# Converting and subtracting w's blocks two at a time, with four moved steps in the prologue

## The chip, the cores and the metric

One core of one Trainium2 chip runs the whole problem in one launch. The metric is the device time of that launch in microseconds (us), as the median of several runs; the profiles are of single executions. Engines: PE is the matmul engine (TensorE), DVE the vector engine, ACT the scalar engine, POOL GpSimd, SP the engine whose queue issues the DMAs.

## The reference

```python
x: (8, 2048, 2048) float32     w: (2048, 2048) float32
cs = np.cumsum(x, axis=1)
diff = cs - (cs shifted by one row, zeros first)     # this is x again
return np.matmul(diff, w).astype(np.float32)
```

A running sum followed by its difference gives x back, so the kernel computes `out = x @ w`: 16384 rows by 2048 columns, with an inner dimension of 2048, float32 in and out.

## The kernel before

**Rows.** The 16384 rows are 128 tiles of 128 rows. Tiles 0 to 3 (`PLAIN = 4`) are multiplied plainly in bf16 while w is still being loaded. From tile 4 on, groups of four tiles (g, g+1, g+2, g+3) go through two nested levels of a Winograd form of Strassen's multiplication in float16, with a scale for each row of x and one for each column half of w. In the code `h = g + 2`; the tiles of the first group are 4 (g), 5, 6 (h) and 7 (h+1).

**w in place.** `W_all` holds all of w in SBUF as 8 rows k of four sections of 1024 float32 numbers. Section `(a, h)` of row k is the half h of the columns of w's row block `ko = 8*a + k`. Once a section is no longer needed in float32, it is scaled by `uinv` and written over itself in float16; that takes half its bytes, so the other half of each section has room for a difference. The four converted blocks are B11, B12, B21, B22, and the differences are T1 = B12 - B11, T2 = B22 - T1, T3 = B22 - B12, T4 = B21 - T2. Each of these eight is 8 pieces, one for each k; before, one DVE instruction made one piece (1024 numbers in each partition): `block` (line 341) for a conversion, line 506 for T1 and `lessen` (line 586) for T2 to T4.

**The prologue.** w's left column half (h = 0) comes first, then the right one (h = 1), each as 16 loads of 512 KB (`fetch`, line 258) on SP's queue. Each block is cast to bf16 on DVE (`cast`, line 266) into a ring of 7 tiles `wb`, and ACT finds its greatest size (`measure`, line 272). PE multiplies tiles 0 to 3 with it (`plain`, line 303). For the left half the order is one block for all four rows at a time up to block 13; then blocks 14 and 15 are done row by row, and each row's sums are copied out of PSUM (`plain_out`, by ACT and DVE in turns). For the right half (`bring(ko)`): load, cast, measure, and behind each a conversion of one piece of B11 or B21 on DVE (`turn_left(1)`); blocks 12 to 15 are done row by row (`finish_row`), with the conversions of B12 in twos between. When `ko` is 10, x's tile 4 is loaded and weighed by ACT (`weigh`), DVE works out its scale (`scale_of`, lines 141 and 143) and ACT narrows it to float16 (`narrow`, line 163). `greatest_of_w(h)` and `scale_of_w(h)` give w's scales by DVE and POOL.

**Around the first group.** `turn` (line 176) transposes a narrowed tile of x by DMA into one of four pairs of tiles `x00 ... x31`; tile 5 goes to `x20, x21`, tile 7 to `x30, x31`. Until then these hold results of the prologue that wait to be stored (`spare`, and `left_over`'s result in `x30`), so their stores come ahead of the transposes. `left_over` (line 457) is the one product of 16 matmuls that the left half leaves out (row 3, second bank). `group_plain` then runs the first group with level-one products of 16 matmuls each; `group_half` and the classes behind it run the second group and all later ones. All later groups follow a list of steps, `ORDER`, written out by hand (`P1.cg` copies a PSUM bank on ACT, `keep.C21h1` scales one bank into an SBUF tile on ACT).

**Order.** `after(engine, ...)` keeps each engine's instructions in the order of the code; engines wait for each other by semaphores that are put in where tiles are shared. A DMA also waits for the DMA eight places ahead of it on SP's queue, since eight semaphores are used in turn.

Of the kernel before, what the change touches and what calls it, by code (L numbers as in the profile page):

```python
# [10 lines left out]
def kernel(  # L11
# [6 lines left out]
    nc = tc.nc  # L18
    P = 128
    B, S, D = x.shape  # L20
# [3 lines left out]
    KO = K // P  # L24
    KH = KO // 2
    NH = N // 2
# [40 lines left out]

    def spare_of(i, k):
        return blocks[:, i // 2, i % 2, ds(k, 2), :, :]

    uw = const.tile([P, 2], f32, name="uw")
    uinv = const.tile([P, 2], f32, name="uinv")
# [9 lines left out]
    def bank(i):  # L82
        return psum.tile([P, NB], f32, name=f"b{i}")
# [101 lines left out]
    with ExitStack() as head:  # L185
# [151 lines left out]
        def block(dst, a, h, k, engine):  # L337
# [5 lines left out]
            else:  # L343
                after(
                    "act", lambda: nc.scalar.activation(dst[k], src, COPY, scale=uinv[:, h : h + 1])
                )

        def dummies(banks):
            for i in banks:
                after(  # L350
                    "pe",
                    lambda: nc.tensor.matmul(
                        bank(i), zeros[:, :P], zeros, start=True, stop=True
                    ),
                )
# [22 lines left out]
            for r in (2 * a, 2 * a + 1):  # L378
                plain(0, r, 0)
        measure(0, 0)  # L380
        for ko in range(1, KO - 2):
            if ko >= EARLY:
                cast(0, ko)
            measure(0, ko)
            q = (ko + 1) // KQ
            turning = ko % KQ == KQ - 1
            if turning:
                xb = cast_x(q)
            for r in range(PLAIN):
                if turning and r in (0, PLAIN - 1):  # L390
                    a = r // 2
                    turned(q, a, turn_x(xb, a, 7), "act")
                plain(0, r, ko)
        for ko in range(KO - 2, KO):
            cast(0, ko)
            measure(0, ko)
        for ko in range(AHEAD):
            fetch(1, ko)
            cast(1, ko)
        for r in range(PLAIN):  # L400
            for ko in range(KO - 2, KO):
                plain(0, r, ko)
            plain_out(0, r)
        greatest_of_w(0)
        for ko in range(AHEAD):
            measure(1, ko)
        ps = [[bank(2 * r + n) for n in here(1, r)] for r in range(PLAIN)]
        left = [(B, a, k) for a, B in enumerate((B11, B21)) for k in range(KH)]

        def turn_left(n):  # L410
            for _ in range(min(n, len(left))):
                B, a, k = left.pop(0)
                block(B, a, 0, k, "dve")

        def bring(ko):
            fetch(1, ko)
            cast(1, ko)
            measure(1, ko)
            if ko == AHEAD:
                scale_of_w(0)  # L420
            turn_left(1)
            if ko == 10:
                load(PLAIN, 0)
                load(PLAIN, 1)
                weigh(PLAIN)
                scale_of(PLAIN)
            if ko == 11:
                narrow(PLAIN)
# [18 lines left out]
        def finish_row(r):  # L447
            for ko in range(KO - KQ, KO):
                plain(1, r, ko)
            plain_out(1, r)  # L450
# [16 lines left out]
            rows = ds((PLAIN - 1) * P, P)  # L467
            after("sp", lambda: put(c, rows, ds(NB, NB), nc.sync))

        turn_left(KH)  # L470
        unit_of(PLAIN)
        turn(PLAIN)
        weigh(PLAIN + 2)
        finish_row(0)
        for k in range(KH):
            block(B12, 0, 1, k, "dve")
            if k == 1:
                scale_of(PLAIN + 2)
            if k % 2:
                if k // 2:  # L480
                    finish_row(k // 2)
        unit_of(PLAIN + 2)
        narrow(PLAIN + 2)
        there = xP.rearrange("p r k m -> p (r k m)")
# [3 lines left out]
        def stores(which):  # L488
            for c, rows, columns in which:
                after("sp", lambda: put(c, rows, columns, nc.sync))  # L490
# [8 lines left out]
        unit_of(PLAIN + 1)  # L499
        narrow(PLAIN + 1)  # L500
        turn(PLAIN + 1)
        stores(done[:3] + done[5:])
        left_over(bank(2))

        for k in range(KH):
            after("dve", lambda: nc.vector.tensor_tensor(T1[k], B12[k], B11[k], SUB))


    class Part:
# [70 lines left out]

    def half_of(t, i):
        return in_twos(t)[:, i]

    def lessen(dst, p, q):
        for k in range(len(dst)):
            after("dve", lambda: nc.vector.tensor_tensor(dst[k], p[k], q[k], SUB))

    def less(dst, p, q):
        if len(dst.shape) == 4 or len(p.shape) == 4 or len(q.shape) == 4:
# [88 lines left out]
    def group_plain(g, X, Y, Z, V):  # L678
        h = g + 2
        lg, lh, kg = (units(t)[0] for t in (g, h, g + 1))  # L680
        ug, uh, vg = (units(t)[1] for t in (g, h, g + 1))
        A11g, A12g = parts(g)
        A11h, A12h = parts(h)
        A21g, A22g = parts(g + 1)
        A21h, A22h = parts(h + 1)
        S1g, S1h = S1
        S2g, S2h, S3g, S3h, S4g, S4h = A11g, A11h, A21g, A21h, A12g, A12h
        load(g + 4, 0)
        load(g + 4, 1)
        product(X, A11g, B11, True)  # L690
        for k in range(3):
            block(B22, 1, 1, k, "act")
        C11g = pair()
        keeps(C11g, X, lg)
        weigh(h + 1)
        for k in range(3, KH):
            block(B22, 1, 1, k, "act" if k < 6 else "dve")
        product(V, A12g, B21, True)
        product(Y, A11h, B11, True)
        lessen(T2[:1], B22[:1], T1[:1])  # L700
        adds(C11g, V, lg)
        puts(C11g, g, 0)
        lessen(T2[1:2], B22[1:2], T1[1:2])
        total(S1g, A21g, A22g, ADD)
        total(S3g, A11g, A21g, SUB)
        total(S2g, S1g, A11g, SUB)
        scale_of(h + 1)
        unit_of(h + 1)
        narrow(h + 1)
        kh, vh = units(h + 1)  # L710
        turn(h + 1)
        lessen(T2[2:], B22[2:], T1[2:])
        product(Z, A12h, B21, True)
        C11h, C22g = (
            [
                inner[:, ds(j, 2), :].rearrange("p a n -> p (a n)").bitcast(f32)
                for j in (i, i + 2)
            ]
            for i in (12, 16)
        )  # L720
        keeps(C11h, Y, lh)
        product(V, S1g, T1, True)
        keeps(C22g, V, vg)
        load(h + 4, 0)
        total(S4g, A12g, S2g, SUB)
        product(X, S2g, T2, False)
        C12g = pair()
        keeps(C12g, X, ug)
        lessen(T3, B22, B12)
        product(V, S4g, B22, False)  # L730
        total(S1h, A21h, A22h, ADD)
        total(S3h, A11h, A21h, SUB)
        total(S2h, S1h, A11h, SUB)
        weigh(g + 4)
        scale_of(g + 4)
        unit_of(g + 4)
        narrow(g + 4)
        load(h + 4, 1)
        turn(g + 4)
        load(g + 5, 0)  # L740
        load(g + 5, 1)
        product(X, S3g, T3, False)
        adds(C11h, Z, lh)
        puts(C11h, h, 0)
        del free[-2:]
        adds(C12g, V, ug)
        puts(C12g, g, 1)
        product(Y, S2h, T2, False)
        C12h = pair()
        keeps(C12h, Y, uh)  # L750
        adds(C22g, X, vg)
        puts(C22g, g + 1, 1)
        del free[-2:]
        total(S4h, A12h, S2h, SUB)
        product(Z, S1h, T1, True)
        weigh(h + 4)
        lessen(T4[:4], B21[:4], T2[:4])
        scale_of(h + 4)
        unit_of(h + 4)
        lessen(T4[4:], B21[4:], T2[4:])  # L760
        C22h = pair()
        keeps(C22h, Z, vh)
        narrow(h + 4)
        weigh(g + 5)
        product(Y, S3h, T3, False)
        in_2.first()
        in_2.fourth()
        load(h + 5, 0)
        load(h + 5, 1)
        turn(h + 4, [0])  # L770
        scale_of(g + 5)
        unit_of(g + 5)
        adds(C22h, Y, vh)
        puts(C22h, h + 1, 1)
        product(Z, S4h, B22, False)
        in_2.third()
        adds(C12h, Z, uh)
        puts(C12h, h, 1)
        narrow(g + 5)
        weigh(h + 5)  # L780
        turn(h + 4, [1])
        turn(g + 5, [0])
        product(X, A22g, T4, False)
        C21 = pair()
        keeps(C21, X, kg)
        puts(C21, g + 1, 0)
        turn(g + 5, [1])
        product(Y, A22h, T4, False)
        less(in_3.Q1, in_3.t12, in_3.t11)
        scale_of(h + 5)  # L790
        unit_of(h + 5)
        C21 = pair()
        keeps(C21, Y, kh)
        narrow(h + 5)
        in_3.second()
        less(in_1.Q1, in_1.t12, in_1.t11)
        turn(h + 5)
        load(g + 8, 0)
        load(g + 8, 1)
        puts(C21, h + 1, 0)  # L800
# [462 lines left out]
    for b in range(-early, len(groups) - late):  # L1263
        for name, ahead in ORDER:
            i = b + ahead
            if 0 <= i < len(groups) and name in groups[i].do:
                if i == len(groups) - 1 and name in END_ORDER:
                    continue
                if i == 1 and name in before:
                    before[name]()  # L1270
                groups[i].do.pop(name)()
                for sooner in SOONER.get(name, ()) if i == len(groups) - 1 else ():
                    groups[i].do.pop(sooner)()
    for name in END_ORDER:
# [32 lines left out]
```

## Time and profile before

| what | before |
|---|---|
| median of 3 runs | 1451.99 us (1451.88 to 1452.24) |
| the profiled execution's own time | 1450.92 us |
| its span, first to last instruction | 1449.1 us |
| PE busy | 1439.1 us (99%), 6686 matmul records |
| DVE busy | 1318.3 us (91%) |
| ACT busy | 971.7 us (67%) |
| POOL busy | 43.5 us (3%) |
| granted PE clock | 1.000 |
| DMA | 351.58 MB, mean 243 GB/s |

Busy is the union of an engine's recorded instructions. A matmul's record lasts 379 ns while matmuls start about 216 ns apart, so PE can lose some 160 ns between two matmuls and still count as busy; short losses are read from the starts. The profiled execution's time is 1.8 us over its span, and 1.07 us under the median.

### The profile page before, as it was taken

What the parts mean: (1) busy time and instruction counts of PE and PEld (TensorE: products, weight loads), DVE (VectorE), ACT (ScalarE), POOL (GpSimd) and SP (SyncE); (2) the same over time, 40 slices, a digit from 0 to 9 for tenths busy, and PEclk for the clock granted to TensorE, in tenths of its full rate; (3) what the DMA queues carried; (4) which work ended last, traced back from release to release, by engine and by line L of the source; (5) the groups of instructions that cost most, each with busy time, mean ns of one, the idle gap of its engine ahead of it and who ended that gap; (6) DMA issues with size and microseconds to landing.
All of it is one profiled execution on the core that took longest, in us unless ns stands there. A gap on an engine that the chain in (4) does not pass through costs nothing.

```text
span 1449.1 us, 20194 instructions
## 1 busy us (share of the span) xinstructions
PE 1439.1 (99%) x6686; PEld 651.7 (45%) x6692; DVE 1318.3 (91%) x2309; ACT 971.7 (67%) x1473; POOL 43.5 (3%) x130
## 2 busy tenths in 40 slices
PE   8999999999999999999999999999999999999998
PEld 4444444444444444444444444444444444444443
DVE  5898899999999999999999999999999999999998
ACT  6987567766666776666666667666667766666662
POOL 0011000000000000000000000000000000000000
PEclk9999999999999999999999999999999999999999
DMA  9999788899888898888898878998878998889973
GB/s 363 371 246 294 202 232 237 234 258 246 231 220 241 243 248 243 231 234 239 248 250 232 235 232 235 263 236 237 228 234 239 253 239 235 224 244 247 254 201 126
DMA packets 378199, 351.58 MB, mean 243 GB/s; under 512 B 274800, under 2 KB 274800, under 8 KB 377968
## 3 DMA queue, kind: packets, MB, share of 16 engines
q1 hardware_dynamic: 378096, 350.31, 86.7%
q8 instruction: 52, 0.85, 0.2%
q14 instruction: 51, 0.42, 0.1%
HBM read 150.99 MB, written 134.22 MB: 197 GB/s over the span
## 4 chain that ended last, share of the span: by engine, by line
PE 93%; DMA 5%; DVE 1%; issue 0%; ACT 0%; SPq 0%; DVEq 0%; ACTq 0%
PE b L623 61%; PE b L604 31%; DMA W<-in_w_dram 4%; DMA x<-F 1%; DVE c L634 1%; PE b L303 0%; DVE x L594 0%; PE b L457 0%; DMA out_dram<-c 0%; DVE wb L266 0%; DVE W L341 0%; ACT c L631 0%; ACT F L163 0%; SPq L224 0%; DVE S L594 0%
## 5 line engine op out<-in xcount | busy, mean ns | idle before, releaser
L634 DVE SCALAR_TENSOR_TENSOR c<-b,of,c 128x512 f32<-128x512 f32 x790 | 573.6, 746 | 70.2 <-PE b L623 60.0
L604 PE MATMUL b<-W,x 128*128 128x512 f16 x2144 | 506.8, 379 | 0.2 <-DVE x L594 0.2
L631 ACT ACTIVATE c<-b,of 128x512 f32<-128x512 f32 x492 | 312.7, 680 | 223.0 <-PE b L623 117.2
L623 PE MATMUL b<-W,x 128*128 128x512 f16 x1904 | 455.0, 379 | 0.1
L163 ACT ACTIVATE F<-F,of 128x1024 f16<-128x1024 f32 x246 | 282.2, 1147 | 175.1 <-DVE of L143 172.9
L623 PEld LDWEIGHTS <-x 128*128 128x128 f16 x2500 | 244.6, 98 | 296.1 <-issue 1.9
L604 PEld LDWEIGHTS <-x 128*128 128x128 f16 x2144 | 209.7, 98 | 253.4 <-DVE x L594 0.7
L124 ACT ACTIVATE waste<-F 128x1024 uint8<-128x1024 f32 x246 | 259.3, 1054 | 8.7 <-DMA F<-in_x_dram 6.6
L623 PEld LDWEIGHTS <-inner 128*128 128x128 f16 x1644 | 160.9, 98 | 194.0 <-issue 0.2
L623 PE MATMUL b<-W,inner 128*128 128x512 f16 x940 | 241.2, 379 | 0.0
L594 DVE TENSOR_TENSOR x<-x,x 128x1024 f16<-128x1024 f16 (+1 forms) x390 | 227.2, 583 | 3.2
L623 PE MATMUL b<-flow,x 128*128 128x512 f16 x588 | 150.9, 379 | 0.1
L623 PE MATMUL b<-inner 128*128 128x512 f16 x472 | 121.1, 379 | 0.0
L947 DVE TENSOR_TENSOR flow<-W 128x2048 f16<-128x2048 f16 x88 | 107.0, 1216 | 0.0
L1040 DVE TENSOR_TENSOR b<-b,c 128x512 f32<-128x512 f32 x116 | 80.5, 694 | 13.4 <-PE b L623 13.4
L149 POOL TENSOR_SCALAR of<-uw,of 128x2 f32<-128x2 f32 x124 | 42.2, 354 | 1301.6 <-DVE of L141 719.3
L947 DVE TENSOR_TENSOR flow<-W,inner 128x2048 f16<-128x2048 f16 x58 | 70.8, 1220 | 0.0
L1033 ACT COPY c<-b 128x512 f32<-128x512 f32 x58 | 33.4, 576 | 52.1 <-PE b L623 46.6
L303 PE MATMUL b<-wb,xP 128*128 128x512 bf16 x234 | 53.5, 379 | 2.8 <-ACT wb L264 1.9
L594 DVE TENSOR_TENSOR inner<-x 128x512 f16<-128x512 f16 x117 | 49.3, 421 | 3.1 <-DMA x<-F 1.1
L1033 ACT COPY b<-b 128x512 f32<-128x512 f32 x87 | 51.2, 588 | 0.0
L594 DVE TENSOR_TENSOR inner<-x,inner 128x512 f16<-128x512 f16 x117 | 49.2, 421 | 2.0
(66 smaller groups left out, 516.6 us busy)
## 6 DMA issues: line engine op xcount, KB each, us to landing
F<-in_x_dram SPq DMA_DIRECT2D x246, 512.0 KB, 5.3
out_dram<-c SPq DMA_DIRECT2D x492, 256.0 KB, 3.1
W<-in_w_dram SPq DMA_DIRECT2D x32, 512.0 KB, 8.4
W<-in_x_dram SPq DMA_DIRECT2D x16, 256.0 KB, 7.8
x<-F SPq DMA_TRANSPOSE x246, 3.4
out_dram<-o SPq DMA_DIRECT2D x5, 256.0 KB, 7.6
out_dram<-wb SPq DMA_DIRECT2D x5, 256.0 KB, 3.5
xP<-in_x_dram SPq DMA_DIRECT2D x1, 1024.0 KB, 6.2
```

The lines of the kernel that those rows point to most:

```text
L124: lambda: nc.scalar.activation(waste, where[t][i], ABS, scale=1.0 / ROW, accum_out=sums_of[t][:, i : i + 1],),
L149: after("pool", lambda: nc.gpsimd.tensor_scalar(u, uw, m, None, MUL))
L163: lambda: nc.scalar.activation(narrowed(t)[:, ds(i * NH, NH)], where[t][i], COPY, scale=s),
L303: lambda: nc.tensor.matmul(ps[r][n], xP[:, r, ko, :], wb[h, ko][:, ds(n * NB, NB)], start=(ko == 0), stop=(ko == KO - 1),),
L594: after("dve", lambda: nc.vector.tensor_tensor(dst.all, p.all, q.all, op))
L604: said = nc.tensor.matmul(to[n], a[k], b[k][:, n, :], start=(first and k == 0), stop=(k == KH - 1), skip_group_check=True,)
L623: said = nc.tensor.matmul(to, a[k], b[k], start=(first and k == 0), stop=(k == 3), skip_group_check=True)
L631: after("act", lambda: nc.scalar.activation(c, p, COPY, scale=u))
L634: after("dve", lambda: nc.vector.scalar_tensor_tensor(c, p, u, c, MUL, ADD))
L947: after("dve", lambda: nc.vector.tensor_tensor(in_twos(flow), x, y, op))
L1033: after("act", lambda: nc.scalar.copy(c, p))
L1040: after("dve", lambda: nc.vector.tensor_tensor(t, p, s, ADD))
```

## The change

1. Conversions of B11, B21, B12 and of B22's last two pieces take two neighbouring k in one DVE instruction (`two_blocks`, 2048 numbers in each partition) instead of one. In `bring`, a pair comes behind every even `ko` (2 to 14) instead of one piece behind each; the last pair stands where the last piece stood.
2. T1, T2, T3 and T4 are made by `minus`, again two k to an instruction. T2's first two pieces are made together ahead of `adds(C11g, ...)`; before, one stood ahead of it and one behind.
3. The left half's row-by-row end starts with block 15 alone; block 14 joins the loop over all rows.
4. For the second group `keep.C21h1` is moved from its place in `ORDER` to right behind `P1.cg` of the third group; both are ACT's.
5. The stores at the end of the prologue: `left_over`'s goes first, then the other one out of an x tile (`done[5]`), then those out of `wb` tiles.

PE's, POOL's and ACT's instructions stay the same in kind and number; DVE makes its 26 conversions in 13 instructions and its 32 differences in 16.

```diff
+    def minus(to, i, j, ks):
+        for k in ks:
+            a, b, c = (spare_of(n, k) for n in (to, i, j))
+            after("dve", lambda: nc.vector.tensor_tensor(a, b, c, SUB))
...
+        def two_blocks(i, a, h, k):
+            src = W_all[:, ds(k, 2), ds((2 * a + h) * NH, NH)]
+            src = src.rearrange("p k (n c) -> p k n c", c=NB)
+            after("dve", lambda: nc.vector.tensor_scalar(
+                spare_of(i, k), src, uinv[:, h : h + 1], None, MUL))
...
-        for ko in range(1, KO - 2):
+        for ko in range(1, KO - 1):
...
-        for ko in range(KO - 2, KO):
+        for ko in range(KO - 1, KO):
             cast(0, ko)
             measure(0, ko)
...
-            for ko in range(KO - 2, KO):
+            for ko in range(KO - 1, KO):
                 plain(0, r, ko)
             plain_out(0, r)
...
-            turn_left(1)
+            if ko % 2 == 0:
+                two_blocks(*left.pop(0))
...
-        turn_left(KH)
+        two_blocks(*left.pop(0))
...
-        for k in range(KH):
-            block(B12, 0, 1, k, "dve")
-            if k == 1:
+        for k in range(0, KH, 2):
+            two_blocks(2, 0, 1, k)
+            if k == 0:
                 scale_of(PLAIN + 2)
...
-        stores(done[:3] + done[5:])
         left_over(bank(2))
-        for k in range(KH):
-            after("dve", lambda: nc.vector.tensor_tensor(T1[k], B12[k], B11[k], SUB))
+        stores(done[5:6] + done[:3] + done[6:])
+        minus(1, 2, 0, range(0, KH, 2))
...
-        for k in range(3, KH):
-            block(B22, 1, 1, k, "act" if k < 6 else "dve")
+        for k in range(3, 6):
+            block(B22, 1, 1, k, "act")
+        two_blocks(6, 1, 1, 6)
...
-        lessen(T2[:1], B22[:1], T1[:1])
+        minus(3, 6, 1, (0,))
         adds(C11g, V, lg)
         puts(C11g, g, 0)
-        lessen(T2[1:2], B22[1:2], T1[1:2])
...
-        lessen(T2[2:], B22[2:], T1[2:])
+        minus(3, 6, 1, (2, 4, 6))
...
+                if groups[i] is half and name == 'keep.C21h1':
+                    continue
...
                 groups[i].do.pop(name)()
+                if groups[i] is first and name == 'P1.cg':
+                    half.do.pop('keep.C21h1')()
```

T3 and T4 change in the same way (`lessen` to `minus`).

More of the change, by code (lines that the diff above doesn't have):

```diff
@@ L346, in block @@
                 )
+        def two_blocks(i, a, h, k):
+            src = W_all[:, ds(k, 2), ds((2 * a + h) * NH, NH)]
+            src = src.rearrange("p k (n c) -> p k n c", c=NB)
+            after(
+                "dve",
+                lambda: nc.vector.tensor_scalar(
+                    spare_of(i, k), src, uinv[:, h : h + 1], None, MUL
+                ),
+            )
         def dummies(banks):
@@ L407 @@
         ps = [[bank(2 * r + n) for n in here(1, r)] for r in range(PLAIN)]
[L408 to L413, printed above, removed]
+        left = [(4 * a, a, 0, k) for a in range(2) for k in range(0, KH, 2)]
         def bring(ko):
@@ L468, in left_over @@
             after("sp", lambda: put(c, rows, ds(NB, NB), nc.sync))
-        turn_left(KH)
+        two_blocks(*left.pop(0))
+        assert not left
         unit_of(PLAIN)
@@ L474 @@
         finish_row(0)
-        for k in range(KH):
-            block(B12, 0, 1, k, "dve")
-            if k == 1:
+        for k in range(0, KH, 2):
+            two_blocks(2, 0, 1, k)
+            if k == 0:
                 scale_of(PLAIN + 2)
-            if k % 2:
-                if k // 2:
-                    finish_row(k // 2)
+            else:
+                finish_row(k // 2)
         unit_of(PLAIN + 2)
@@ L582, in half_of @@
         return in_twos(t)[:, i]
-    def lessen(dst, p, q):
-        for k in range(len(dst)):
-            after("dve", lambda: nc.vector.tensor_tensor(dst[k], p[k], q[k], SUB))
     def less(dst, p, q):
@@ L728, in group_plain @@
         keeps(C12g, X, ug)
-        lessen(T3, B22, B12)
+        minus(5, 6, 2, range(0, KH, 2))
         product(V, S4g, B22, False)
@@ L756, in group_plain @@
         weigh(h + 4)
-        lessen(T4[:4], B21[:4], T2[:4])
+        minus(7, 4, 3, (0, 2))
         scale_of(h + 4)
         unit_of(h + 4)
-        lessen(T4[4:], B21[4:], T2[4:])
+        minus(7, 4, 3, (4, 6))
         C22h = pair()
```

## The prediction

> **What bounds the kernel now.** I read the page's first part and the shares of its chain, then PE by stages, then PE's starts wherever it is late.
>
> ```profile
> span 1449.1 us, 20194 instructions
> ...
> PE 1439.1 (99%) x6686; PEld 651.7 (45%) x6692; DVE 1318.3 (91%) x2309; ACT 971.7 (67%) x1473; POOL 43.5 (3%) x130
> ...
> PE 93%; DMA 5%; DVE 1%; issue 0%; ACT 0%; SPq 0%; DVEq 0%; ACTq 0%
> ```
>
> ```profile
> 9.20:38.00 28.80, 27.32 (x159) 12.92 (x162) 15.26 (x22) 23.90 (x38) 0.00 (x0) 1.00 1.03 403
> 38.00:191.00 153.00, 152.41 (x700) 68.50 (x702) 136.69 (x230) 116.33 (x174) 12.77 (x14) 1.00 0.95 274
> 191.00:1444.00 1253.00, 1253.00 (x5806) 567.80 (x5803) 1161.30 (x2046) 829.11 (x1261) 30.50 (x112) 1.00 0.86 235
> ```
>
> PE bounds it. From 191 us to 1444 us it is never idle, and no edit but the moved copy and keep lies past 140 us. So the change is worth what it moves PE at about 191 us; from there every group follows at PE's pace. All that PE idles between 9.2 and 191 us is 1.48 + 0.59 = 2.07 us (plus short losses hidden in the pipelined records). Measurement of this kernel can tell about 0.2% (2.9 us) from no change: a gain of that size isn't there to be had by these edits. A loss has no such limit.
>
> Where PE is late, and the pace it is measured with:
>
> ```profile
> 200.89 18.13 PE b L623 x84
> ```
>
> ```profile
> 35.68 1.67 PE L303 MATMUL b<-wb,xP 128*128 128x512 bf16 x7
> 37.59 6.63 PE L303 MATMUL b<-wb,xP 128*128 128x512 bf16 x29 [0.24 <-DVE wb L266]
> ...
> 85.35 3.63 PE L604 MATMUL b<-W,S 128*128 128x512 f16 x16
> ...
> 96.80 2.54 PE L604 MATMUL b<-W,x 128*128 128x512 f16 x11
> 99.50 1.68 PE L604 MATMUL b<-W,x 128*128 128x512 f16 x7 [0.16 <-DVE x L594]
> ```
>
> 18.13/84 = 0.216 us a matmul. From 35.68 to 37.59 seven matmuls take 1.91 us, so 1.91 - 1.51 = 0.40 us is lost before the left half's last block; from 96.80 to 99.50 eleven take 2.70, so 0.33 is lost before the product S2h x T2.
>
> **Part 3, the left half's end.** The loss at 37.59 is row 0 waiting for the cast of block 15 after its two matmuls with block 14. With block 14 done for all rows there are five more matmuls (1.08 us) to run in that time: the 0.40 us goes. It is not kept, as the next part shows.
>
> **Part 1 up to the right half's last block.**
>
> ```profile
> 56.29 0.21 DVE L141 TENSOR_SCALAR of<-of 128x1 f32<-128x1 f32 x1 [2.18 <-ACT waste L124]
> ...
> 56.62 0.69 DVE L266 CAST wb<-W 128x1024 bf16<-128x1024 f32 x1
> 57.22 0.75 DVE L341 TENSOR_SCALAR W<-W,uinv 128x1024 f16<-128x1024 f32 x1
> ...
> 61.68 0.69 DVE L266 CAST wb<-W 128x1024 bf16<-128x1024 f32 x1
> ```
>
> ```profile
> 61.77 0.61 DVE wb L266
> ...
> 62.42 1.67 PE b L303 x7
> ```
>
> ```profile
> 60.51 0.19 ACT L272 ACTIVATION_READ_ACCUMULATOR waste<-W 128x1 f32 x1
> ```
>
> At 56.29 DVE has stood idle for 2.18 us until ACT had weighed tile 4, so nothing saved on DVE before that arrives behind it. From there to the cast of block 15 (61.68), which releases PE at 62.42, are four casts and four single conversions; afterwards four casts and two pairs.
>
> The price of a pair is not in the trace. Near rows are single conversions, one or two in a row, and the differences in float16 with 1024 and 2048 numbers:
>
> ```profile
> 65.20 0.73 DVE L341 TENSOR_SCALAR W<-W,uinv 128x1024 f16<-128x1024 f32 x1
> ...
> 66.45 1.41 DVE L341 TENSOR_SCALAR W<-W,uinv 128x1024 f16<-128x1024 f32 x2
> ...
> 68.10 1.40 DVE L341 TENSOR_SCALAR W<-W,uinv 128x1024 f16<-128x1024 f32 x2
> 69.41 0.69 DVE L333 COPY x<-b 128x512 f32<-128x512 f32 x1
> ```
>
> ```profile
> 74.18 4.89 DVE L506 TENSOR_TENSOR W<-W 128x1024 f16<-128x1024 f16 x8
> ...
> 84.60 0.69 DVE L594 TENSOR_TENSOR S<-x,x 128x1024 f16<-128x1024 f16 x1 [1.67 <-DMA x<-xP]
> ```
>
> ```profile
> L947 DVE TENSOR_TENSOR flow<-W 128x2048 f16<-128x2048 f16 x88 | 107.0, 1216 | 0.0
> ```
>
> Back to back a single difference takes 4.89/8 = 0.61, and the second 1024 numbers add 1.216 - 0.69 = 0.53, so a pair takes 1.14 and saves 0.08. A single conversion takes 0.66 back to back (two in a row 1.41, one 0.75); a pair, with the same 0.53 added, 0.66 + 0.53 = 1.19. Ends: 1.32 if nothing is saved, 1.14 if it is as quick as a pair of differences. I take 1.19, as the instruction itself (0.75 against 0.69) is that near to the rows.
>
> The Trainium skill, "VectorE: DVE Perf Modes", section "The TRN2 errata — SBUF-src ops pay a fixed extra latency per instruction", has about 150 cycles of fixed cost in each instruction, an estimated 0.16 us at its 0.96 GHz. By it a pair would take 1.15; the sum below would be 0.1 us lower. The rows show less, as neighbours overlap.
>
> Now the sum: casts at 56.62 and 57.22, a pair from 57.83 to 59.02, casts to 60.23. The second pair writes rows whose span in the tile takes in the right half's block 12, so in the built program it waits until ACT has measured that block: 60.51 + 0.19 = 60.70. It runs from 60.74 to 61.93, and the cast of block 15 starts at 61.93 instead of 61.68: PE is **0.25 us later**, and the 0.40 us gained before is used up by waiting. Without that wait the cast would start at 61.42 (0.26 earlier); with pairs of 1.32, 0.38 later.
>
> **Part 1 up to the first group's products.** To the DVE rows from 65.20 on come SP's:
>
> ```profile
> 70.12 1.16 SPq L313 DMA_DIRECT2D out_dram<-x  x2
> ...
> 76.80 5.72 SPq L176 DMA_TRANSPOSE x<-xP  x2
> ...
> 90.99 4.17 SPq L176 DMA_TRANSPOSE x<-F  x2
> ```
>
> Before the copy at 69.41 stand five single conversions, afterwards three pairs, since one piece more comes after 65.20: 3 x 1.19 - 5 x 0.66 = **0.27 us later** (0.12 to 0.66). SP's next store waits for that copy (69.41 + 0.69 = 70.10, issued 70.12). Behind it queue tile 6's transposes, tile 7's loads and tile 5's transposes (76.80), whose landing ends DVE's 1.67 us of idleness at 84.60; the sum made there releases PE at 85.35 (84.60 + 0.69 = 85.29). So S1g x T1 starts 0.27 later, at 85.62. PE by itself would be there 0.25 late, so this wait decides by a little.
>
> Over all five pairs DVE is 5 x 1.19 - 9 x 0.66 = 0.01 later, T1 then saves 8 x 0.61 - 4 x 1.14 = 0.32, T2 to T4 0.08 a pair: all this lies in the 1.67 us of idleness, and is worth nothing. If that cover went, PE would wait for S1g on DVE instead, no later than before. T1 to T4 in twos come at most one piece (0.6 us) late for the matmul that reads the first; they are finished before their products start or run 0.6 ahead of PE, which needs one k every 0.43 us.
>
> **Part 5, the stores.** The loss at 99.50 hangs on tile 7:
>
> ```profile
> 97.23 0.69 DVE L594 TENSOR_TENSOR S<-x,x 128x1024 f16<-128x1024 f16 x1 [1.14 <-DMA x<-F]
> ```
>
> ```profile
> 84.00:97.00 13.00, 13.00 (x61) 5.80 (x60) 11.39 (x20) 11.13 (x15) 1.37 (x1) 1.00 1.08 304
> ```
>
> Tile 7's transposes are issued at 90.99, and wait for `left_over`'s store, the last of seven. With that store first they can be issued behind SP's two stores of C, about 1.8 us sooner. But from 84 to 97 us the DMA engines are busy without a break (1.08), with the same seven stores, two loads and two stores of C ahead of the transposes either way. I expect them to land no sooner relative to tile 5's, so, with tile 5, 0.27 late: S2h is ready 0.27 later, PE at 99.77. PE alone would come at 85.62 + 64 x 0.216 = 99.44.
>
> The Trainium skill, "DMA: Bandwidth & Descriptors", section "Queues, rings and completion order", says that each DMA engine takes a ring's descriptors in their order; by it an early issue waits behind the same transfers, and the time is the one I take.
>
> **Part 4, the copy ahead of the keep.**
>
> ```profile
> 163.96 0.69 ACT L631 ACTIVATE c<-b,of 128x512 f32<-128x512 f32 x1 [0.77 <-DVE c L634]
> 164.55 0.59 ACT L1033 COPY b<-b 128x512 f32<-128x512 f32 x1
> ```
>
> ```profile
> 165.19 2.97 PE b L623 x13
> ```
>
> `keep.C21h1` waits for DVE until 163.96, and the copy behind it, ready long before, releases PE at 165.19. In the 0.77 us of ACT's idleness ahead of the keep there is room for the copy's 0.59, so it is done before 163.96, PE isn't held, and the keep is no later than now. PE's matmuls would otherwise follow at 164.97: **0.22 us gained**.
>
> **Sum.** +0.27 from the first group, -0.22 at 165 us: +0.05. What lies between (DVE, DMA and ACT steps at 120 to 160 us) follows PE. The profiled execution has 1450.92 us; it would be 1451.0. The median shown is 1.07 over it, so the forecast is 1451.99 + 0.05 = 1452.0.
>
> **Rivals.** *Transposes land sooner.* If the early issue does bring tile 7 forward, the 0.33 us at 99.50 goes: PE is at 99.44 instead of 99.50, and -0.06 - 0.22 = -0.28 gives 1451.7; if the pairs cost nothing at 62 us and on the way to tile 5 either, PE is at 85.35 as now, then at 99.16 without a wait, and -0.34 - 0.22 = -0.56 gives 1451.4. For it: the issue is plainly held now. Against: the DMA share.
>
> *Loads of w are held.* In the built program the loads of the right half's blocks 8, 10, 12 and 14 wait for DVE's pairs, since a pair's span covers their place.
>
> ```profile
> 36.74 4.17 SPq L258 DMA_DIRECT2D W<-in_w_dram  x4
> ```
>
> ```profile
> 36.74 10.19 DMA W<-in_w_dram
> ```
>
> ```profile
> F<-in_x_dram SPq DMA_DIRECT2D x246, 512.0 KB, 5.3
> ...
> W<-in_w_dram SPq DMA_DIRECT2D x32, 512.0 KB, 8.4
> ```
>
> ```profile
> 41.98 0.75 DVE L341 TENSOR_SCALAR W<-W,uinv 128x1024 f16<-128x1024 f32 x1
> ```
>
> The four issues from 36.74, one each 1.3 us, are blocks 7 to 10. The first pair comes one cast later than the first conversion now (41.98 + 0.61), so it ends at 43.8, and block 8, issued near 38.0 now, goes out at 43.9. The load of block 7 lands at 46.93, so the DMA engines have work for 3 us more. With the page's median of 5.3 us for a load of x of the same size, block 8 would land at 49.2, against 46.93 + 1.3 = 48.2 now. Its cast comes at 50 us, and the last block could be 1 us late without being missed (cast at 61.93). If a held load took the 8.4 us of the page's w loads, all would land 4 us late, block 15 near 63.9, and PE would be 2.2 us late: 1454.2. It decides from a delay of about 2 us.
>
> *Pairs lose DVE's fast pace (slower).* If the conversion with one dimension more ran at half the pace, a pair would take 1.19 + 1.07 = 2.26: three pairs ahead of 69.41 cost 6.78 - 3.30 = +3.5, all of it on tile 5, and the end is 3.5 - 0.22 = +3.3, 1455.3. It decides as soon as a pair is over 1.4. Nothing in the profile shows such a conversion.
>
> By the Trainium skill's "VectorE: DVE Perf Modes", section "What auto-detection actually checks", a one-source instruction in SBUF keeps the double pace if the outermost dimensions of both sides are even or equal; here both are 2, so this rival would not happen.
>
> **Numbers.** Forecast as summed 0.58, transposes sooner 0.27, loads held 0.10, half pace 0.03, unnamed 0.02. The forecast's own ends are 1451.9 to 1452.4 (pairs of 1.14 to 1.32); the first rival reaches down to 1451.4, less 0.4 for the spread of the runs shown; upward, half of the held loads is taken in. Range 1451.0 to 1453.2. Faster by over 0.2%: 0.03, as 2.07 us of idleness doesn't hold it; slower by over 0.2%: 0.07 (half pace, the worst of held loads, unnamed); within: 0.90.
>
> **What would show it.** Right: pairs of about 1.28 us on their own; no loss at 37.59, but PE held by the cast of block 15 near 62.7; x's store at 70.4; S1g's sum at 84.9; tile 7's transposes issued near 89 and landed near 97.4; no wait at 165. Wrong: tile 7 landed before 96.5, pairs over 1.4 us, block 8 landed after 50, or a new idle stretch of PE over 0.5 us anywhere past 38 us.

## The result, and the profile after

| | median | runs | |
|---|---|---|---|
| before | 1452.16 us | 22 | 1451.04 to 1452.88 |
| after | 1453.82 us | 22 | 1452.22 to 1455.48 |

The ratio of after to before is 1.0013, 95% interval [1.0007, 1.0019]: some 1.9 us slower (1.0 to 2.8; the medians are 1.66 us apart). The forecast of 1452.0 and its range (to 1453.2) missed it. The profiled execution took 1454.19 us (1450.92 before).

Of the page after, the span, the engines' busy time, and the chain by engine:

```profile
span 1452.1 us, 20165 instructions
...
PE 1439.1 (99%) x6686; PEld 651.4 (45%) x6692; DVE 1316.0 (91%) x2280; ACT 971.8 (67%) x1473; POOL 45.4 (3%) x130
...
PE 91%; DMA 5%; DVE 1%; ACT 1%; issue 1%; SPq 0%; DVEq 0%; POOL 0%; ACTq 0%
```

PE's busy time by stages, after:

```profile
9.20:38.00 28.80, 26.53 (x158) 12.67 (x160) 15.05 (x22) 23.55 (x36) 0.00 (x0) 1.00 1.03 404
38.00:191.00 153.00, 150.25 (x687) 67.02 (x688) 131.37 (x198) 113.72 (x171) 14.67 (x14) 1.00 0.95 272
191.00:1444.00 1253.00, 1253.00 (x5806) 567.92 (x5805) 1161.55 (x2046) 831.47 (x1265) 30.51 (x112) 1.00 0.87 235
```

PE does the same work in the same 1439.1 us. From 191 us on it never idles, as before. Between 38 and 191 us it idles 2.75 us where it idled 0.59: these 2.16 us are the loss. (The 0.79 us more up to 38 us differ from execution to execution: runs below with the same code there have 26.4 to 27.5.)

Where it comes from stands in the chain of waits after, in order of time (start, length, what):

```profile
45.58 1.21 DVE W L358
46.80 0.33 SPq L263
...
48.23 9.07 DMA W<-in_w_dram
...
63.03 0.70 DVE wb L271
63.77 1.67 PE b L308 x7
...
65.50 1.99 PE b L308 x9
67.49 6.66 DMA xP<-in_x_dram
...
79.45 6.59 DMA x<-xP
...
86.95 0.70 DVE S L600
...
87.70 5.95 PE b L610 x27
```

A pair of `two_blocks` (L358) ends, and what it releases is SP's queue: the load of block 10. The chain then runs through the DMA queue: w's late blocks, the cast of block 15 (63.03 instead of 61.68), PE's rows behind that cast, x5 (the load of tile 5 of x into `xP`), tile 5's transposes, S1g, and S1g x T1 at 87.70 instead of 85.35. x5 waits for PE, which reads `xP` up to 67.49 (65.50 + 1.99); SP's queue comes free for it only 0.1 us sooner, at 67.40, when it has issued tile 4's transposes. So both roads, PE's and the queue's, are late by about as much. The second rival happened. SP's waits between 36 and 64 us (total, times, longest) after:

```profile
SPq L263 <- DVE W L358: 9.3, 4, 5.9
```

Before, no load waited for DVE. The last two columns of these rows are the DMA engines' busy share and GB/s; first before, then after:

```profile
44.00:48.00 4.00, 4.00 (x21) 1.81 (x19) 4.00 (x7) 3.89 (x8) 0.00 (x0) 1.00 1.03 404
50.00:53.00 3.00, 3.00 (x15) 1.36 (x14) 3.00 (x6) 2.91 (x7) 0.00 (x0) 1.00 1.02 408
```

```profile
44.00:48.00 4.00, 4.00 (x20) 1.81 (x19) 4.00 (x7) 3.91 (x7) 0.00 (x0) 1.00 0.91 293
50.00:53.00 3.00, 3.00 (x15) 1.37 (x14) 2.53 (x4) 2.94 (x5) 0.00 (x0) 1.00 0.95 277
```

The engines still count as busy at 0.91 and 0.95, but move a quarter to a third less: (404 - 293) x 4 + (408 - 277) x 3 = 837 KB, at 408 GB/s 2.05 us of transfer that is missing. In slices of 1 us, after:

```profile
45.00:46.00 1.00, 1.00 (x6) 0.49 (x5) 1.00 (x2) 1.00 (x2) 0.00 (x0) 1.00 0.76 217
46.00:47.00 1.00, 1.00 (x7) 0.42 (x5) 1.00 (x2) 0.97 (x3) 0.00 (x0) 1.00 0.93 274
47.00:48.00 1.00, 1.00 (x6) 0.47 (x5) 1.00 (x3) 0.97 (x3) 0.00 (x0) 1.00 1.00 303
```

Block 8, held, is issued at 44.41, and block 7 lands only at 47.39. Yet from 45 us on the engines have already partly run out of work (0.76); then they are busy again, but slow. By the trace's landings block 15 comes 15.02 us after block 7 (47.39 to 62.41); before it was 12.80 (46.93 to 59.73): a lag of 2.2 us.

### The profile page after: what moved, and what is told of

It is laid out like the page before. It is cut to its first block, busy times and chain, and to the rows that moved or that the text cites. A ratio compares the mean times of both kernels' runs of the same rounds, so it can differ in the third digit from the quotient of the medians.

```text
span 1452.1 us, 20165 instructions
## 1 busy us (share of the span) xinstructions
PE 1439.1 (99%) x6686; PEld 651.4 (45%) x6692; DVE 1316.0 (91%) x2280; ACT 971.8 (67%) x1473; POOL 45.4 (3%) x130
## 4 chain that ended last, share of the span: by engine, by line
PE 91%; DMA 5%; DVE 1%; ACT 1%; issue 1%; SPq 0%; DVEq 0%; POOL 0%; ACTq 0%
PE b L629 61%; PE b L610 30%; DMA W<-in_w_dram 2%; DMA x<-F 1%; PE b L308 1%; DMA F<-in_x_dram 1%; DMA xP<-in_x_dram 0%; DMA x<-xP 0%; DMA W<-in_x_dram 0%; ACT waste L129 0%; DVE x L600 0%; DVE c L640 0%; ACT F L168 0%; ACT c L637 0%; DVE wb L271 0%
## 5 line engine op out<-in xcount | busy, mean ns | idle before, releaser
L600 DVE TENSOR_TENSOR inner<-x,inner 128x512 f16<-128x512 f16 x117 | 49.2, 421 | 2.0
```

What stands on the lines that cost most here:

```text
L600: after("dve", lambda: nc.vector.tensor_tensor(dst.all, p.all, q.all, op))
```

## Experiments

Each is told with its median against the kernel before on the same chip (1451.5 to 1451.6 there).

### Is it the holds, the pairs' price, or another edit?

**Single conversions again.** The changed kernel with this edit:

```diff
-            if ko % 2 == 0:
-                two_blocks(*left.pop(0))
+            turn_left(1)
...
-        two_blocks(*left.pop(0))
+        turn_left(KH)
```

> The changed kernel with the sixteen conversions of the left half (B11, B21) made one row at a time again, in the old places; the five other edits stay. Held loads (theory): no load of w waits for DVE, block 8 is issued at 38 us again and block 15 lands at 59.7; the end is where the kernel before is, less the 0.22 us of the moved keep: 1452.0, and within 0.5 us of it. Rival, the differences in twos or the order of the stores are what costs: still 1453.5 or more.

1451.49 against 1451.61, ratio 1.0 [0.9991, 1.0008]. Without the pairs, and so without the holds, the loss is gone.

**Pairs alone**: the reverse edit in the kernel before, nothing else changed.

> The kernel before with one edit: the left half's conversions in twos. Held loads: the whole loss is there, block 8 issued near 44.4 us, block 15 landed near 62.4, PE 1.35 us late for the cast of block 15 and about 2.3 at S1g x T1; 1453.8 to 1454.1 (the moved keep's gain is missing). Rival, other edits cost: 1452.2.

1453.79, ratio 1.0015 [1.0006, 1.0024]: the whole loss.

**Pairs of one row**, which hold no load:

```diff
-                two_blocks(*left.pop(0))
+                two_of_row()
...
+        left = list(range(KH))
+        def two_of_row():
+            k = left.pop(0)
+            src = whole[k][:, :, 0, :].rearrange("p a (n c) -> p a n c", c=NB)
+            dst = pieces[k][:, 0:3:2, 0]
+            after("dve", lambda: nc.vector.tensor_scalar(dst, src, uinv[:, :1], None, MUL))
```

> The changed kernel, but each pair is the two left-half blocks of one row of the tile (B11[k] with B21[k]) in place of two rows: as many conversions of 2048 numbers, and their span takes in only the right half's block k, loaded long before. Held loads: no load waits for DVE; 1451.7 to 1452.4. Rival, the pairs' own price on DVE (1.28 us alone, DVE stalling behind them): 1453.5 to 1454, as changed.

1451.50, ratio 1.0 [0.9992, 1.0009]. Its DVE rows and its DMA rate:

```profile
57.89 1.28 DVE L430 TENSOR_SCALAR W<-W,uinv 128x2048 f16<-128x2048 f32 x1
59.09 1.29 DVE L271 CAST wb<-W 128x1024 bf16<-128x1024 f32 x2
60.29 1.28 DVE L430 TENSOR_SCALAR W<-W,uinv 128x2048 f16<-128x2048 f32 x1
```

```profile
44.00:48.00 4.00, 4.00 (x20) 1.82 (x19) 4.00 (x6) 3.90 (x8) 0.00 (x0) 1.00 1.03 401
50.00:53.00 3.00, 2.95 (x14) 1.37 (x14) 3.00 (x4) 2.91 (x7) 0.00 (x0) 1.00 1.04 414
```

As many pairs, each as long (1.28 us) as in the changed kernel, and no loss: the pairs' price is not it.

**The span alone**: the kernel before, each conversion half a block of two rows.

```diff
-                B, a, k = left.pop(0)
-                block(B, a, 0, k, "dve")
+                i, a, k, n = left.pop(0)
+                src = W_all[:, ds(k, 2), ds(2 * a * NH + n * NB, NB)]
+                dst = blocks[:, i // 2, i % 2, ds(k, 2), n, :]
+                after("dve", lambda: nc.vector.tensor_scalar(dst, src, uinv[:, :1], None, MUL))
```

> The kernel before, but each single conversion takes half a block of two rows (2 x 512 numbers) in place of one block: as many instructions of as many numbers as before, no pairs, yet the span of two rows. Held loads: blocks 8, 10, 12 and 14 wait for DVE, block 8 is issued near 45 us, and the time is 1453.8 to 1455. Rival, the pairs' price: 1452.2, as before.

1453.22, ratio 1.0011 [1.0002, 1.0020]; GB/s 293 and 254 in the two stretches. No pair, and still the loss (a little under the expected 1453.8). These four settle it: with the two-row span it is slow, with pairs or without; without the span it is not, with pairs or without.

### Which hold, and how long may it be?

In the texts below, F(4) is the load of tile 4 of x and T(4) its transposes.

**One hold, two holds.** The changed kernel, but only the first, or the first two, conversions are pairs; the others are single.

```diff
-            if ko % 2 == 0:
-                two_blocks(*left.pop(0))
+            if ko in (2,):          # two holds: (2, 4)
+                two_blocks(0, 0, 0, left.pop(0)[1])
+                left.pop(0)
+            elif ko > 2:            # two holds: 4
+                turn_left(1)
```

> The changed kernel, but of the left half's conversions only the first (rows 0 and 1 of B11) is a pair; the other fourteen are single. Only block 8 of w waits for DVE. As the prediction reckoned (block 8 about 1 us late at most, the last block's slack takes that up): block 8 lands 0.7 us late, PE not late, 1451.3 to 1451.9. Rival, the lag runs on through the queue: F(4), block 15, T(4) and tile 5 all land 0.6 to 0.7 us late, and the end is 0.4 to 0.7 us late, 1452.0 to 1452.3.

> As the run with one pair, but with the first two conversions as pairs: blocks 8 and 10 wait for DVE, 12 and 14 don't. If the lag is made by the first two holds, as the landings after the change suggest (0.66 us at block 8, 1.79 at block 10, 2.69 at F(4), 2.68 from there on): all of the loss, 1453.3 to 1454, and block 15 lands near 62.4. Rival, each of the four holds adds its part: about half, 1452.4 to 1452.9.

1453.52, ratio [1.0007, 1.0025], and 1453.48 [1.0003, 1.0020]. One hold, of block 8, costs as much as all four, within what can be told. Both theories of the first run had it too small, the prediction's by most.

**Only blocks 12 and 14; only block 10.** The same form, with rows 4 to 7, or rows 2 and 3, of B11 as pairs.

> The changed kernel, but only the third and fourth conversions (rows 4 to 7 of B11) are pairs, so blocks 12 and 14 wait for DVE, 8 and 10 don't. Drained queue (theory): eight loads stand in the queue and one lands 10.2 us after its issue; a load issued into an empty queue lands 4.5 to 5.4 us after it. So a hold shorter than 5 us is not seen by the DMA engines; these two are held about 3.5 us (to 49.2 and 51.6, from 45.7 and 48.2), and cost nothing: 1451.3 to 1451.9. Rival, every hold leaves its lag: 1452.3 or more.

> The changed kernel, but only the second conversion (rows 2 and 3 of B11) is a pair, so block 10 alone waits for DVE, from 40.6 to about 46.8, 6.2 us as block 8 does in the run with one pair. Drained queue: the hold is 1 us or so longer than the queue lasts, block 15 lands 1 to 1.5 us late, 1453 to 1453.7. Rival, the first held load is a special one: 1451.5.

1451.47 [0.9989, 1.0006] and 1454.57 [1.0012, 1.0030]. Late holds are free; block 10 alone costs 1.7 to 4.4 us, 3 by the medians, more than expected. SP's waits and the DMA rate, first with blocks 12 and 14 held, then with block 10:

```profile
SPq L263 <- DVE W L358: 4.9, 2, 3.4
```

```profile
50.00:53.00 3.00, 3.00 (x16) 1.34 (x15) 3.00 (x5) 2.90 (x7) 0.00 (x0) 1.00 1.03 410
```

```profile
SPq L263 <- DVE W L358: 6.0, 1, 6.0
```

```profile
50.00:53.00 3.00, 3.00 (x16) 1.36 (x14) 3.00 (x5) 2.94 (x6) 0.00 (x0) 1.00 0.97 258
54.00:57.00 3.00, 3.00 (x15) 1.36 (x14) 0.81 (x4) 2.90 (x7) 0.00 (x0) 1.00 1.01 314
```

A hold of 3.4 us leaves the rate at 410; one of 6.0 us brings it to 258, and it has not recovered 8 us after block 10 went out at 46.88 (314 GB/s from 54 to 57).

**Tile 4's loads between**, to give the engines work during the holds; once in the changed kernel, once in the one with two holds:

```diff
         def bring(ko):
+            if ko == 8:
+                load(PLAIN, 0)
+                load(PLAIN, 1)
             fetch(1, ko)
...
             if ko == 10:
-                load(PLAIN, 0)
-                load(PLAIN, 1)
                 weigh(PLAIN)
```

> The changed kernel with all its pairs and holds, but tile 4's two loads of x are issued ahead of block 8 of w in place of behind block 10. They wait for nothing and give the DMA engines 2.6 us more work during the first hold. Drained queue: no gap, block 15 lands about 12.8 us after block 7 as in the kernel before (15.0 after the change), 1451.4 to 1452.2. Rival, a held load costs by itself, or the pairs do: 1453.3 to 1454.

> The run with two pairs (blocks 8 and 10 held), with tile 4's two loads issued ahead of block 8, so that both blocks' turns come 2.6 us later and the holds last 3.7 us in place of 6.2. Drained queue: GB/s stays near 405 from 44 to 58 us and nothing is lost, 1451.4 to 1452.0. Rival, a held load costs however long: 1453 or more, as the run with two holds (1453.5).

The first: 1453.98 [1.0007, 1.0025], against the theory at first sight. But its rate holds much longer (397 GB/s still from 53 to 58 us), and falls only then:

```profile
50.00:53.00 3.00, 3.00 (x16) 1.35 (x15) 1.72 (x2) 2.36 (x5) 0.00 (x0) 1.00 1.03 412
...
58.00:61.00 3.00, 3.00 (x16) 1.35 (x15) 3.00 (x5) 2.97 (x5) 0.00 (x0) 1.00 0.94 242
```

Block 8 lands behind tile 4's halves, so its cast is late on DVE; the pair that holds block 14 stands behind that cast, and block 14 goes out at 53.20. The second has only the two early holds:

```profile
44.00:48.00 4.00, 4.00 (x21) 1.77 (x19) 4.00 (x6) 3.87 (x9) 0.00 (x0) 1.00 1.03 404
50.00:53.00 3.00, 3.00 (x16) 1.35 (x15) 2.18 (x4) 2.34 (x5) 0.00 (x0) 1.00 1.03 412
```

The rate holds, there is no lag, and 1452.59, ratio 1.0007 [0.9998, 1.0016]. That is neither the 1451.4 to 1452.0 of the theory nor the rival's 1453 or more, and with these intervals the medians can't show that it is quicker than the same holds without the loads between (1453.48); what is shown is that the loads keep their rate. Two things make this execution late without a lag: block 7 already lands 0.92 us later than in the kernel before (47.85 and 46.93), and block 8's late landing makes the later measures and casts late (the last one releases PE here after 0.67 us of idleness):

```profile
63.96 5.77 PE L308 MATMUL b<-wb,xP 128*128 128x512 bf16 x26 [0.67 <-DVE wb L271]
```

From the issues and landings in the traces, with the microseconds of loads still queued ahead (up to the landing of the last of them) when the held ones were issued; the last column is the time of the execution that the row is read from:

| kernel | queued ahead at the held issues | block 7 to 15 | lag | us |
|---|---|---|---|---|
| before | none held | 12.80 | | 1450.92 |
| after | 3.0, 3.3, then over 8 | 15.02 | 2.2 | 1454.19 |
| pairs alone | 3.1, 3.7, then over 8 | 15.19 | 2.4 | 1455.47 |
| span alone | 2.7, 3.6, then over 7 | 15.14 | 2.3 | 1453.83 |
| one hold | 2.9 | 14.33 | 1.5 | 1452.30 |
| two holds | 3.0, 4.0 | 14.59 | 1.8 | 1453.48 |
| block 10 | 3.7 | 14.89 | 2.1 | 1453.53 |
| loads between, four holds | 5.5, 5.7, 5.9, 4.3 | 14.05 | 1.3 | 1453.15 |
| loads between, two holds | 5.6, 5.8 | 12.74 | 0 | 1452.57 |
| blocks 12 and 14 | 5.6, 5.8 | 12.88 | 0.1 | 1450.30 |
| pairs of one row | none held | 12.88 | 0.1 | 1451.80 |
| differences alone (below) | none held | 13.48 | 0.7 | 1451.99 |

Where every held load was issued with 5.5 us or more queued ahead, the loads land 1.28 us apart. With 4.3 us or less there is a gap, and some of the loads behind it come 1.5 to 3.1 us apart until the queue is long again; with block 10 held, block 9, the load ahead of it, is slow too (2.07 us). A gap can come without a hold: in the last row block 8 lands 1.95 us behind block 7, with 9.2 us queued ahead. Each row is one execution, up to 1.7 us off the median of its kernel (one hold: 1452.30 and 1453.52).

### By what road does the lag reach the end?

**More loads**: the kernel before with one, or two, loads of 512 KB more ahead of block 8; no hold, no pair.

```diff
         def bring(ko):
+            if ko == 8:
+                load(PLAIN + 2, 0)    # two more: load(PLAIN + 2, 1) too
             fetch(1, ko)
```

> The kernel before with one more load of 512 KB in SP's queue ahead of block 8 of the right half (the first half of tile 6 of x, into the place where it is loaded again later). Nothing is held; the queue is 1.28 us longer from there on. As the prediction reckoned (block 15 may be 1 us late without being missed): 1451.5 to 1451.8. Lag of the queue (theory): tile 5's transposes and S1g x T1 come 1.0 to 1.3 us later, 1452.5 to 1452.9.

> The same with two more loads, both halves of tile 6, 2.56 us of queue. By the cast of block 15 alone (lands at 62.3, cast at 63.05): PE 0.7 to 0.8 us late there, 1452.3. Lag of the queue: 2.3 to 2.6 us, 1453.8 to 1454.1, as much as the change itself.

1453.13 [1.0002, 1.0020] and 1453.40 [1.0004, 1.0022]. With one, block 15 lands 1.29 us later (61.02). SP's queue, before and with one load more, and PE with one load more:

```profile
58.51 6.21 SPq L176 DMA_TRANSPOSE x<-F  x2
64.81 0.53 SPq L487 DMA_DIRECT2D xP<-in_x_dram  x1
```

```profile
59.81 6.13 SPq L176 DMA_TRANSPOSE x<-F  x2
66.03 0.53 SPq L489 DMA_DIRECT2D xP<-in_x_dram  x1
```

```profile
59.79 8.38 PE L303 MATMUL b<-wb,xP 128*128 128x512 bf16 x37
...
86.78 3.63 PE L606 MATMUL b<-W,S 128*128 128x512 f16 x16 [1.29 <-DVE S L596]
```

PE runs through block 15 without a gap (starts there are 0.23 us late, as before), but x5's load goes out at 66.03 instead of 64.81, and S1g x T1 starts at 86.78 instead of 85.35. So a lag of the queue costs by itself, behind block 15. Two loads cost less than the expected 2.3 to 2.6 us, and the two runs can't be told apart; in the trace x5 goes out 1.64 us later than with one, but S1g x T1 starts only 0.30 later (87.08).

The execution of "differences alone" shows the same road with nothing done to the loads: after its gap block 15 lands 1.10 us later than in the kernel before (60.83), S1g x T1 starts 1.09 later (86.44), and it takes 1.07 us more. Over all seventeen profiled executions, S1g x T1 starts 24.5 to 26.3 us after block 15 has landed, and the time is 1364.8 to 1366.5 us more than that start.

### Two small terms, and a try for more

**The copy ahead of the keep, alone** in the kernel before:

```diff
+                if groups[i] is half and name == 'keep.C21h1':
+                    continue
...
+                if groups[i] is first and name == 'P1.cg':
+                    half.do.pop('keep.C21h1')()
```

> The kernel before with one edit, the copy ahead of the keep. As predicted: 0.22 us less, 1451.4 on the side of the kernel before's 1451.6, and no wait of PE between 163 and 180 us. Rival, given back: the 0.22 us at 165 go, and five us later PE waits 0.2 to 0.4 us for DVE's sum into a bank (b from b and c): 1451.6 to 1451.8.

1451.56, as before, ratio 1.0 [0.9992, 1.0009]; 0.22 us is too little for this interval either way. PE's wait at 165 us is gone, and there is a new one, for DVE's sum into a bank:

```profile
160.51 6.28 PE L623 MATMUL b<-W,x 128*128 128x512 f16 x28
...
170.86 1.02 PE L623 MATMUL b<-W,inner 128*128 128x512 f16 x4 [0.61 <-DVE b L1040]
```

```profile
170.11 0.69 DVE L1040 TENSOR_TENSOR b<-b,c 128x512 f32<-128x512 f32 x1
```

It isn't shown that the edit makes this sum late: DVE is behind by 0.57 us from 157.72 on (157.15 before), ahead of the moved copy. In the executions with two holds and with blocks 12 and 14 held, which have this edit too, PE has no wait at either place.

**The differences alone** (T1 to T4 by `minus`) in the kernel before:

> The kernel before with one edit, the differences T1 to T4 in twos. As predicted, worth nothing: 1451.4 to 1451.8. Rival, a difference of two pieces holds DVE 1.2 us at a time and lets a sum or a keep come late near 131 us: PE waits 0.3 us there where it waited 0.04, 1451.9.

1451.48, ratio 0.9999 [0.9990, 1.0008]: nothing that can be told, as predicted, and no wait near 131 us.

**Scale one block later**, on the kernel with single conversions:

```diff
                 weigh(PLAIN)
-                scale_of(PLAIN)
             if ko == 11:
+                scale_of(PLAIN)
                 narrow(PLAIN)
```

> A try for a better kernel: the run with single conversions and all the other edits, and tile 4's scale on DVE one block later, so that DVE does not stand idle 2.2 us ahead of the last casts. The cast of block 15 comes at 60.5 instead of 61.7 and PE's 0.6 us loss before the right half's last block goes. If what follows (tile 5's transposes, tile 7's) hangs on the DMA queue, PE waits there instead and 0 to 0.3 us are left: 1451.2 to 1451.5; if on PE, 1450.9.

1452.06, ratio 1.0003 [0.9994, 1.0012]. The wait for block 15's cast goes, PE then waits 0.12 us at S1g x T1 and 0.31 at S2h x T2, and the time is no better. No version here beats the kernel before by anything that can be measured.

## Why the prediction was wrong, step by step

- **Pairs' price, right.** 1.28 us alone (forecast about 1.28), and 1.20 us from a pair's start to the next instruction's (57.89 to 59.09; I took 1.19; the other estimate, 1.32 - 0.16, is 1.16 and not the 1.15 that I wrote). Half pace did not happen: the Trainium skill's rule on even outer dimensions ("VectorE: DVE Perf Modes", "What auto-detection actually checks") agrees with the 1.28 us of the trace.
- **The left half's end, right.** The 0.40 us at 37.59 are gone. With single conversions and no holds PE gives 0.29 back in a new wait at 43.77 and 0.10 more at block 15.
- **Up to the first group, right for the kernel that I had priced.** With pairs that hold nothing, x's store goes out at 70.46 (70.4 forecast), and S1g x T1 starts at 85.71 (85.62).

```profile
70.46 1.17 SPq L318 DMA_DIRECT2D out_dram<-x  x2
```

```profile
85.71 3.63 PE L618 MATMUL b<-W,S 128*128 128x512 f16 x16 [0.44 <-DVE S L608]
```

- **The stores, right.** With single conversions tile 7's transposes are issued at 89.20 instead of 90.99, and land at 97.12 instead of 97.14: 1.8 us sooner out, nothing sooner in. The order of a ring's descriptors (the Trainium skill, "DMA: Bandwidth & Descriptors", "Queues, rings and completion order") agrees with that.

```profile
89.20 5.94 SPq L181 DMA_TRANSPOSE x<-F  x2
```

- **The copy ahead of the keep: the wait went as forecast, the 0.22 us aren't shown as gained.** I did not ask what is late next. In the run with that edit alone it is DVE's sum into a bank (b from b and c), done only at 170.80 (170.11 and 0.69), which holds PE for 0.6 us; in other executions with the edit that wait is shorter or isn't there.
- **The sum, without the holds, agrees, but proves little.** +0.05 us was forecast; the kernel with pairs of one row and all other edits measures 1451.50 against 1451.61, with an interval of some 1.2 us to either side. Neither of the sum's terms, 0.27 and 0.22, could be seen in it.
- **The step that failed is the price of "Loads of w are held".** The rival was named, with its blocks, queue and issue time (43.9; it was 44.41), and block 8 itself came even closer behind block 7 than priced (1.5 us, where 49.2 - 46.93 = 2.3 had been put). Two things in its price were wrong. I took the delay to be block 8's own: the queue had "work for 3 us more", and I let everything behind block 8 follow at the full rate. But 3 us up to a landing were not 3 us of work: after the change block 8 went out 3.0 us before block 7 landed, and the engines were busy 0.76 of the time from 45 to 46 us. The loads then ran at 293 and 277 GB/s and had lost 2.2 us by block 15; one such hold alone loses 1.5. And I followed the lag only to the cast of block 15, where it may be 1 us late for nothing. That last sentence was true, as the run with one more load shows. But the queue goes on behind block 15, to tile 4's transposes, x5 and tile 5's transposes, and my own part 1 had S1g x T1 hang on their landing. So "it decides from a delay of about 2 us" should have been "a lag of this queue costs from the first microsecond on": in their traces one load more, 1.28 us, moved S1g x T1 by 1.43, and two moved it by 1.73. The rival's 0.10 was far too low: the holds were in the built program, and only their price was in doubt. My own sign for it, block 8 landed after 50, stayed silent (48.86), since it watched block 8 and not the loads behind it; the sign that did show was PE's idleness of over 0.5 us (1.21 us at the cast of block 15).
- **What measurement can tell, put too coarse.** I took 0.2% as the least that can be told; 22 runs of each kernel tell 0.13% from no change.

Three things stay open. Why the loads stay slow for some microseconds when the queue has run short was not tested. Why the second load more costs so little is not known. And block 10 held alone has the highest median of all, 1454.57, but its interval overlaps those of the other held kernels, and its profiled execution (1453.53, S1g x T1 at 87.57) is no later than the changed kernel's (1454.19, 87.70); that it costs more than the others is not shown.

## What to carry to other kernels

In the built program an access pattern over two rows of a tile can hold a load whose data it doesn't touch: look up, for every instruction that is widened, what its whole span covers, and who waits for that. In a stretch where the DMA engines are busy without a break, price a late load by the lag of the queue up to the last transfer that anyone waits for, not by the first reader of the late block. A wait that is removed counts as a gain only when it is known which engine is late next.

## What the hardware showed that was not expected

Loads that have still to land are not all work that has still to be done. In this prologue each load of 512 KB takes 1.28 us when the held ones are issued with 5.5 us or more of loads ahead, counted up to their landing. With 3.0 us ahead the DMA engines partly run out (0.76 busy, 217 GB/s, from 45 to 46 us after the change), and with 4.3 us or less the rate stays low for some microseconds behind it. The busy share hides most of that: 0.91 to 1.01 at 242 to 314 GB/s in the stretches of 3 and 4 us above, against 1.03 at 404. GB/s shows it. In the traces' packets of 4096 B the mean goes from 163 ns (before, 50 to 53 us) to 222 ns (after, same stretch), 244 (block 10 held) and 253 (loads between, four holds, 58 to 61 us), while the median stays at 159 to 162: most packets are as quick as ever, and a tenth take over 350 ns.
